# Low parts of the unsummed weight blocks: from a subtraction on VectorE to a negated copy on ScalarE and an accumulating DMA

## The chip, the cores and the metric

The kernel runs on one core of one Trainium2 chip. The metric is device time in microseconds (us) from the first to the last instruction of one execution, taken over several runs; lower is better. A change of about 0.2% is the least that a measurement of this kernel can tell from no change.

## The reference, cut to what matters

Two layers of a hybrid diffusion backbone over 512 latent and 256 context tokens, model width 1024. Each layer is a gated feed-forward network (FFN, inner width 2816), a mixing block (neighbourhood attention, windowed attention and a Fourier part between one input and one output projection), and a second FFN. Every dense product is in float32:

```python
def swiglu(h, w1, w2):
    gate, up = jnp.split(h @ w1, 2, axis=-1)
    return (jax.nn.silu(gate) * up) @ w2

def hybrid_layer(x, xc, mod, mod_c, ...):
    x = ffn_sublayer(x, mod, 0, ...)             # xc likewise
    ...                                          # mixing: h @ w_in, three mixers, o @ w_out
    x = ffn_sublayer(x, mod, 2, ...)
```

The weights are w1 (1024 x 5632) and w2 (2816 x 1024) of four FFNs, w_in (1024 x 2048) and w_out (1024 x 1024) of two layers, and w_mod, which gives the modulation rows.

## The kernel before, in words

TensorE multiplies in a reduced float32 format (fp32r). To keep float32 accuracy, each operand is split in two: the high part is the value rounded to fp32r, the low part is the value less its high part. A product is then three matmuls: high by high, high by low, low by high (`mm`, L693 is the line of the profile for all of them).

Weights stream through on-chip memory. `weights()` has two threads. `loads()` has the DMA queue of SP bring one weight tile of 128 x 1024 (512 KB) after another into one of 2 buffers `raw` (a third joins once the modulation rows are done). `split()` takes them in the same order and makes of each two blocks of 128 x 512. A block needs one of 8 slots (`W_BUFS`); a slot is two tiles, `wh` and `wl`. `block()` has ScalarE (ACT) copy the block into `wh`, rounded (L324), and `low()` has VectorE (DVE) subtract `wh` from the block into `wl` (L328); then `raw` may be loaded anew, and TensorE (PE) may use the block. The slot comes free when PE's last matmul with the block is done.

Most of the first projection of each FFN (77 of 88 column pairs, weights of the name "ws") uses a scheme with 7 products in place of 8 (`sums()`, `pair7()`). Its pair of tiles gives 7 blocks: three are parts of the weights themselves (a11, a12, a22), four are sums and differences (s1 to s4), which VectorE first writes into tiles `q` (L333). So VectorE and ScalarE convert 861 blocks in all: 308 from `q` and 553 straight from `raw` (3 of each of the 77 pairs, and all blocks of w2, w_in, w_out, the 11 other pairs of w1 and the Fourier tables). The blocks of the first modulation weights (32, L459 and L460) are converted elsewhere.

The order of all instructions on every engine is made by a planner (`Sched`) when the program is built: each step has an engine, an assumed duration and, for transfers, an assumed time until its result may be used (the last argument of `op`), and the step that could start first is put next. Engines then run their lists in order; an instruction that waits holds up all behind it on its engine. Slots and buffers are counted resources (`acq`, `rel`).

Other work that the change touches by sharing an engine: GpSimd (POOL) computes 1/sqrt of the norm (`rstd`, L547) at each start of a sublayer, and issues no DMA. ScalarE evacuates PSUM banks, computes silu (L935, L943) and makes the high parts of activations (L667). VectorE adds partial products (L1023), reduces the modulation rows from `wmodT` tiles (L433, which come by SP's queue, L427) and makes low parts of activations (L668). Ten small transfers (`gsd`, L533) turn a column of 1024 values into a row in DRAM.

Of the kernel before, what the change touches and what calls it, by code (L numbers as in the profile page):

```python
# [13 lines left out]
AF = mybir.ActivationFunctionType  # L14
ALU = mybir.AluOpType
# [143 lines left out]
def op(eng, dur, fn, extra=0.0):  # L159
    return ("op", eng, dur, fn, extra)  # L160


def wait(ev):
    return ("wait", ev)


def acq(name, n=1):
    return ("acq", name, n)


def t_dve(n, ap=False):
    return n / 960.0 + (0.13 if ap else 0.07)


def t_act(n, ap=False):
    return n / 1200.0 + (0.18 if ap else 0.09)
# [6 lines left out]
class Prog:  # L183
# [111 lines left out]
    def weights(self):  # L295


        nc, S = self.nc, self.S
        its = self.items()
        self.W = {}  # L300
        for k, _ in its:
            if k[0] == "ws":
                self.W.update({(*k, b): Event() for b in BLOCKS})
            else:
                self.W[k] = [Event() for _ in range(self.halves(k))]
        loaded = [[Event() for _ in aps] for _, aps in its]

        def loads():
            yield wait(self.start_w)
            for (key, aps), evs in zip(its, loaded):  # L310
                for ap, ev in zip(aps, evs):
                    yield acq("raw_w")
                    raw = self.rawp.tile([128, 1024], F32, name="raw")
                    n = 512 * self.halves(key)
                    yield op("sp", 1.45 * n / 1024, lambda: nc.sync.dma_start(out=raw[:, :n], in_=ap), 2.0)
                    S.set(ev, raw)

        def slot():
            wh = self.wp.tile([128, 512], F32R, name="wh")
            wl = self.wp.tile([128, 512], F32R, name="wl")  # L320
            return wh, wl

        def block(src, w, ev, after):
            yield op("act", t_act(512), lambda: nc.scalar.activation(w[0], src, AF.Copy))  # L324
            S.spawn(low(src, w, ev, after), 0)

        def low(src, w, ev, after):
            yield op("dve", t_dve(512), lambda: nc.vector.tensor_tensor(w[1], src, w[0].bitcast(F32), ALU.subtract))  # L328
            after()
            S.set(ev, w)  # L330

        def tt(o, a, b, f):
            return op("dve", t_dve(512), lambda: nc.vector.tensor_tensor(o, a, b, f))  # L333

        def sums(key, evs):
            rg = yield wait(evs[0])
            left = {0: 4, 1: 2}

            def done(*which):
                for r in which:  # L340
                    left[r] -= 1
                    if left[r] == 0:
                        S.rel("raw_w")

            a11, a12 = rg[:, :512], rg[:, 512:]
            W = lambda n: self.W[(*key, n)]
            yield acq("w")
            yield from block(a11, slot(), W("a11"), lambda: done(0))
            yield acq("w")
            yield from block(a12, slot(), W("a12"), lambda: done(0))  # L350
            ru = yield wait(evs[1])
            a21, a22 = ru[:, :512], ru[:, 512:]
            yield acq("q")
            s1 = self.qp.tile([128, 512], F32, name="q")
            yield tt(s1, a21, a22, ALU.add)
            yield acq("q")
            s2 = self.qp.tile([128, 512], F32, name="q")
            yield tt(s2, s1, a11, ALU.subtract)
            yield acq("w")
            yield from block(s1, slot(), W("s1"), lambda: S.rel("q"))  # L360
            yield acq("q")
            s4 = self.qp.tile([128, 512], F32, name="q")
            yield tt(s4, a12, s2, ALU.subtract)
            done(0)
            yield acq("w")
            yield from block(s2, slot(), W("s2"), lambda: S.rel("q"))
            yield acq("w")
            yield from block(s4, slot(), W("s4"), lambda: S.rel("q"))
            yield acq("q")
            s3 = self.qp.tile([128, 512], F32, name="q")  # L370
            yield tt(s3, a11, a21, ALU.subtract)
            done(0, 1)
            yield acq("w")
            yield from block(s3, slot(), W("s3"), lambda: S.rel("q"))
            yield acq("w")
            yield from block(a22, slot(), W("a22"), lambda: done(1))

        def split():
            for (key, _), evs in zip(its, loaded):
                if key[0] != "ws":  # L380
                    raw = yield wait(evs[0])
                    n = self.halves(key)
                    for i in range(n):
                        yield acq("w")
                        after = (lambda: S.rel("raw_w")) if i == n - 1 else (lambda: None)
                        yield from block(raw[:, i * 512 : i * 512 + 512], slot(), self.W[key][i], after)
                    continue
                yield from sums(key, evs)

        S.spawn(loads(), 0)  # L390
        S.spawn(split(), 0)

    @staticmethod
# [1458 lines left out]
```

## Time and profile before

| | us |
|---|---|
| median of 3 runs | 2574.09 |
| lowest and highest run | 2572.94, 2575.4 |
| the profiled execution | 2578.36 |
| its span, first to last instruction | 2576.6 |
| PE busy | 2518.8 (98%) |
| DVE busy | 1957.9 (76%) |
| ACT busy | 1266.8 (49%) |
| POOL busy | 68.1 (3%) |

The profile is of one execution. Busy time of an engine leaves out the time that it spends on waits and on issuing DMAs. PE is busy in every slice of the span but the first; that says that it always has a matmul under way, not that it could not be quicker. All later rows give times from the start of the span.

### The profile page before, as it was taken

How to read it: one execution, taken by the hardware profiler on the slowest of the kernel's cores; microseconds unless marked ns; L12 is line 12 of the kernel's file. 1: busy time of each engine (PE TensorE's matmuls, PEld its weight loads, DVE VectorE, ACT ScalarE, POOL GpSimd, SP SyncE). 2: the span in 40 equal slices, each digit the busy share in tenths (PEclk: the TensorE clock that was granted, in tenths of full speed). 3: DMA queues.
4: the chain of work that ended last, by engine and by line, in shares of the span. 5: the costliest groups of instructions: out<-in, count | busy, mean ns of one | idle time of the engine just before them, and what ended most of it. 6: DMA issues, size and time to landing. Idle time of an engine off the chain costs nothing.

```text
span 2576.6 us, 40296 instructions
## 1 busy us (share of the span) xinstructions
PE 2518.8 (98%) x15304; PEld 2291.8 (89%) x15304; DVE 1957.9 (76%) x3906; ACT 1266.8 (49%) x2529; POOL 68.1 (3%) x136
## 2 busy tenths in 40 slices
PE   7999999999999999999999999999999999999998
PEld 5989998998887899998999999899999877899998
DVE  7878888886888397887887968666667577768887
ACT  8433333356557474333334743333347566654544
POOL 0000000010000000000000100000001000000000
PEclk9999999999999999999999999999999999999999
DMA  6333434353321324344447344222243221333334
GB/s 255 95 119 123 127 121 103 117 196 102 123 62 34 123 86 129 121 131 107 123 123 201 118 156 155 75 74 69 71 154 112 69 68 67 114 115 91 99 107 131
DMA packets 100931, 294.17 MB, mean 114 GB/s; under 512 B 20608, under 2 KB 27136, under 8 KB 100608
## 3 DMA queue, kind: packets, MB, share of 16 engines
q1 hardware_dynamic: 100736, 291.59, 36.7%
q8 instruction: 120, 1.97, 0.3%
q14 instruction: 75, 0.61, 0.1%
HBM read 274.73 MB, written 16.82 MB: 113 GB/s over the span
## 4 chain that ended last, share of the span: by engine, by line
PE 90%; DVE 3%; DMA 3%; ACT 2%; issue 1%; SPq 0%; POOL 0%; DVEq 0%; POOLq 0%; ACTq 0%
PE b L693 82%; PE b L1345 3%; PE b L1388 2%; PE b L1324 2%; DMA raw<-wmodT 1%; PE b L675 1%; DMA raw<-w 1%; DVE wl L328 1%; ACT wh L324 1%; DMA raw<-win 1%; DMA g<-wmod 0%; DVE q L433 0%; ACT y L661 0%; DVE wl L460 0%; PE b L1134 0%
## 5 line engine op out<-in xcount | busy, mean ns | idle before, releaser
L693 PE MATMUL b<-hh,wh 128*128 128x256 f32 (+2 forms) x2184 | 703.4, 322 | 18.1 <-ACT q L935 13.2
L693 PE MATMUL b<-hl,wh 128*128 128x256 f32 (+2 forms) x2184 | 686.8, 318 | 1.7 <-DVE hl L668 1.4
L693 PE MATMUL b<-hh,wl 128*128 128x256 f32 (+2 forms) x2184 | 667.5, 318 | 0.0
L693 PE MATMUL b<-wh,g 128*128 128x512 f32 x1936 | 606.9, 390 | 0.0
L328 DVE TENSOR_TENSOR wl<-raw,wh 128x512 fp32r<-128x512 f32 x553 | 367.0, 689 | 132.1 <-ACT wh L324 129.7
L324 ACT ACTIVATE wh<-raw 128x512 fp32r<-128x512 f32 x553 | 336.4, 627 | 233.4 <-PE b L693 177.9
L693 PEld LDWEIGHTS b<-hh,wh 128*128 128x128 f32 x2184 | 414.4, 190 | 39.5 <-ACT q L935 14.2
L693 PEld LDWEIGHTS b<-wh,g 128*128 128x128 f32 x1936 | 363.6, 188 | 73.9
L693 PEld LDWEIGHTS b<-hl,wh 128*128 128x128 f32 x2184 | 414.4, 190 | 14.5 <-DVE hl L668 2.7
L693 PEld LDWEIGHTS b<-hh,wl 128*128 128x128 f32 x2184 | 402.4, 190 | 3.0
L324 ACT ACTIVATE wh<-q 128x512 fp32r<-128x512 f32 x308 | 190.5, 629 | 418.5 <-DVE y L1023 248.9
L693 PE MATMUL b<-wl,g 128*128 128x512 f32 x968 | 377.3, 390 | 0.0
L433 DVE CUSTOM_DVE_ANT_0 q<-raw,cb 128x1024 bf16<-128x1024 f32 x224 | 273.5, 1221 | 55.7 <-DMA raw<-wmodT 54.7
L693 PE MATMUL b<-x,wh 128*128 128x384 f32 (+1 forms) x1232 | 292.3, 323 | 0.0
L328 DVE TENSOR_TENSOR wl<-q,wh 128x512 fp32r<-128x512 f32 x308 | 206.3, 688 | 73.2 <-ACT wh L324 72.1
L1023 DVE TENSOR_TENSOR y<-y,b 128x512 f32<-128x512 f32 x264 | 179.6, 685 | 101.3 <-PE b L693 99.7
L693 PEld LDWEIGHTS b<-x,wh 128*128 128x128 f32 x1232 | 215.1, 189 | 0.0
L693 PEld LDWEIGHTS b<-wl,g 128*128 128x128 f32 x968 | 181.8, 188 | 35.8
L693 PE MATMUL b<-x,wl 128*128 128x384 f32 (+1 forms) x616 | 198.6, 322 | 0.0
L693 PE MATMUL b<-g,wh 128*128 128x384 f32 (+1 forms) x616 | 148.6, 327 | 4.3 <-ACT s L935 4.3
L961 ACT ACTIVATE g<-s 128x384 fp32r<-128x384 f32 (+1 forms) x154 | 75.5, 494 | 95.2 <-DVE s L948 94.1
L693 PEld LDWEIGHTS b<-x,wl 128*128 128x128 f32 x616 | 116.2, 189 | 0.0
(258 smaller groups left out, 3219.9 us busy)
## 6 DMA issues: line engine op xcount, KB each, us to landing
raw<-w SPq DMA_DIRECT2D x264, 512.0 KB, 3.6
raw<-wmodT SPq DMA_DIRECT2D x128, 512.0 KB, 3.6
raw<-win SPq DMA_DIRECT2D x32, 512.0 KB, 3.6
spill<-x SPq DMA_DIRECT2D x28, 512.0 KB, 2.9
x<-spill SPq DMA_DIRECT2D x26, 512.0 KB, 7.0
g<-wmod SPq DMA_DIRECT2D x32, 256.0 KB, 5.4
raw<-wout SPq DMA_DIRECT2D x16, 512.0 KB, 3.6
y<-bias SPq DMA_DIRECT2D x24, 256.0 KB, 3.1
```

What stands on the lines that cost most here:

```text
L324: yield op("act", t_act(512), lambda: nc.scalar.activation(w[0], src, AF.Copy))
L328: yield op("dve", t_dve(512), lambda: nc.vector.tensor_tensor(w[1], src, w[0].bitcast(F32), ALU.subtract))
L433: yield op("dve", t_dve(1024, True), lambda: nc.vector.tensor_tensor_reduce(junk, raw, self.cb[:, i, :], 1.0, 0.0, ALU.mult, ALU.add, self ...
L675: r = nc.tensor.transpose(bank[:, c : c + 128], yb[:, t, 2 * j + i, :], self.ident)
L693: mm = lambda *a, **k: self.nc.tensor.matmul(*a, skip_group_check=onto, **k)
L961: yield op("act", t_act(N), lambda: nc.scalar.activation(gh, ts[h], AF.Copy))
L1023: yield op("dve", t_dve(512), lambda: nc.vector.tensor_tensor(dst, dst, p, ALU.add))
L1324: r = nc.tensor.transpose(pb[:, j * 128 : j * 128 + 128], P[:, b * 128 : b * 128 + 128], self.ident)
L1345: r = nc.tensor.matmul(ps[b][:, c : c + w], lhsT=q[x], rhs=k[x], start=x == 0, stop=x == 1)
L1388: r = nc.tensor.matmul(po["t"][64 * h : 64 * h + 64, cols], lhsT=vs[h][j], rhs=Ps[h][:, j * 128 : j * 128 + 128], start=(j == 0), stop=(j ...
```

## The change

For the 553 blocks that come straight from `raw`, ScalarE makes a second copy, negated, into `wl`. The DMA queue of POOL then brings the same 128 x 512 values out of DRAM again and adds them onto `wl` (128 rows of 2 KB; an accumulating DMA). VectorE no longer takes part in these blocks. `raw` is released after the second copy. The 308 blocks from `q` stay as they are.

```diff
+        def added(src, ap, w, ev, after):
+            yield op("act", t_act(512), lambda: nc.scalar.activation(w[0], src, AF.Copy))
+            yield op("act", t_act(512), lambda: nc.scalar.activation(w[1], src, AF.Copy, scale=-1.0))
+            after()
+            S.spawn(add(ap, w, ev), 0)
+        def add(ap, w, ev):
+            yield op("pool", 1.0, lambda: nc.gpsimd.dma_start(out=w[1], in_=ap, accum_op=ALU.add), 2.5)
+            S.set(ev, w)
...
-        def sums(key, evs):
+        def sums(key, aps, evs):
...
-            yield from block(a11, slot(), W("a11"), lambda: done(0))
+            yield from added(a11, aps[0][:, :512], slot(), W("a11"), lambda: done(0))
...
-            yield from block(a12, slot(), W("a12"), lambda: done(0))
+            yield from added(a12, aps[0][:, 512:], slot(), W("a12"), lambda: done(0))
...
-            yield from block(a22, slot(), W("a22"), lambda: done(1))
+            yield from added(a22, aps[1][:, 512:], slot(), W("a22"), lambda: done(1))
...
-                        yield from block(raw[:, i * 512 : i * 512 + 512], slot(), self.W[key][i], after)
+                        cols = slice(i * 512, i * 512 + 512)
+                        yield from added(raw[:, cols], aps[0][:, cols], slot(), self.W[key][i], after)
```

## Rows read from the trace of the kernel before

**Rows 1.** The page's head and its first part: span, busy time by engine.

```profile
span 2576.6 us, 40296 instructions
PE 2518.8 (98%) x15304; PEld 2291.8 (89%) x15304; DVE 1957.9 (76%) x3906; ACT 1266.8 (49%) x2529; POOL 68.1 (3%) x136
```

**Rows 2.** Windows of 50 us: busy PE, PEld, DVE, ACT, POOL; clock, DMA share, GB/s.

```profile
250.00:300.00 50.00, 50.00 (x257) 45.74 (x256) 42.98 (x73) 16.27 (x30) 0.00 (x0) 1.00 0.38 115
1700.00:1750.00 50.00, 50.00 (x256) 45.75 (x256) 30.95 (x50) 16.80 (x31) 0.00 (x0) 1.00 0.22 64
```

**Rows 3.** The chain that ended last, shares by line (the answer cuts the line off).

```profile
by line: PE b L693 82.2%; PE b L1345 2.7%; PE b L1388 1.9%; PE b L1324 1.8%; DMA raw<-wmodT 1.2%; PE b L675 1.0%; DMA raw<-w 0.9%; issue 0.8%; DVE wl L328 0.6%; ACT wh L324 0.5%; DMA raw<-win 0.5%; DMA g<-wmod 0.4%; DVE q L433 0.4%; ACT y L
```

**Rows 4.** Costliest groups: the two conversions; busy us, mean ns, idle before.

```profile
L328 DVE TENSOR_TENSOR wl<-raw,wh 128x512 fp32r<-128x512 f32 x553 | 367.0, 689 | 132.1 <-ACT wh L324 129.7
L324 ACT ACTIVATE wh<-raw 128x512 fp32r<-128x512 f32 x553 | 336.4, 627 | 233.4 <-PE b L693 177.9
```

**Rows 5.** Waits: who waited for whom, us in total, times, longest.

```profile
SPq L315 <- DVE wl L328: 768.7, 198, 27.1
ACT wh L324 <- PE b L693: 243.9, 208, 9.5
```

**Rows 6.** Timeline: start, duration; ACT's conversions, then PE's matmuls with the low parts.

```profile
533.12 0.63 ACT L324 ACTIVATE wh<-raw 128x512 fp32r<-128x512 f32 x1 [1.18 <-DMA raw<-w]
563.56 1.99 ACT L324 ACTIVATE wh<-raw 128x512 fp32r<-128x512 f32 x3 [0.39 <-PE b L693]
570.33 1.14 ACT L324 ACTIVATE wh<-raw 128x512 fp32r<-128x512 f32 x2
873.64 0.63 ACT L324 ACTIVATE wh<-raw 128x512 fp32r<-128x512 f32 x1 [0.29 <-PE b L693]
1426.10 1.99 ACT L324 ACTIVATE wh<-raw 128x512 fp32r<-128x512 f32 x3 [0.48 <-PE b L693]
2548.39 0.63 ACT L324 ACTIVATE wh<-raw 128x512 fp32r<-128x512 f32 x1 [0.82 <-DMA raw<-w]
...
537.34 0.39 PE L693 MATMUL b<-wl,g 128*128 128x512 f32 x1
568.36 0.28 PE L693 MATMUL b<-hh,wl 128*128 128x256 f32 x1
574.01 0.28 PE L693 MATMUL b<-hh,wl 128*128 128x256 f32 x1
878.51 0.40 PE L693 MATMUL b<-wl,hh 128*128 128x512 f32 x1
1430.90 0.28 PE L693 MATMUL b<-hh,wl 128*128 128x256 f32 x1
2550.92 0.39 PE L693 MATMUL b<-wl,g 128*128 128x512 f32 x1
```

**Rows 7.** DMA: the queue's packets, MB, share; issues: count, KB each, us to landing.

```profile
q1 hardware_dynamic: 100736, 291.59, 36.7%
...
raw<-w SPq DMA_DIRECT2D x264, 512.0 KB, 3.6
...
y<-bias SPq DMA_DIRECT2D x24, 256.0 KB, 3.1
q<-gsd SPq DMA_DIRECT2D x20, 256.0 KB, 6.5
```

**Rows 8.** Timeline: one DMA issue of SP, two operations of POOL on one column.

```profile
562.37 0.32 SPq L640 DMA_DIRECT2D spill<-x  x1
...
570.59 0.86 POOL L547 TENSOR_TENSOR R<-r,nhalf 128x1 f32<-128x1 f32 x1 [9.82 <-DVE r L543]
573.14 2.74 POOL L547 TENSOR_TENSOR R<-r,nhalf 128x1 f32<-128x1 f32 x1 [1.69 <-DVE r L545]
```

**Rows 9.** Timeline of DVE: a late modulation row; a scaling of 1024 columns.

```profile
424.52 1.23 DVE L433 CUSTOM_DVE_ANT_0 q<-raw,cb 128x1024 bf16<-128x1024 f32 x1 [5.94 <-DMA raw<-wmodT]
...
572.19 0.75 DVE L635 TENSOR_SCALAR y<-x,R 128x1024 f32<-128x1024 f32 x1
```

More of the change, by code (lines that the diff above doesn't have):

```diff
@@ L375, in sums @@
             yield acq("w")
-            yield from block(a22, slot(), W("a22"), lambda: done(1))
+            yield from added(a22, aps[1][:, 512:], slot(), W("a22"), lambda: done(1))
         def split():
-            for (key, _), evs in zip(its, loaded):
+            for (key, aps), evs in zip(its, loaded):
                 if key[0] != "ws":
@@ L385, in split @@
                         after = (lambda: S.rel("raw_w")) if i == n - 1 else (lambda: None)
-                        yield from block(raw[:, i * 512 : i * 512 + 512], slot(), self.W[key][i], after)
+                        cols = slice(i * 512, i * 512 + 512)
+                        yield from added(raw[:, cols], aps[0][:, cols], slot(), self.W[key][i], after)
                     continue
-                yield from sums(key, evs)
+                yield from sums(key, aps, evs)
         S.spawn(loads(), 0)
```

## The prediction

> **What bounds the kernel now.** I read the busy times first, then the windows, the chain of waits, and last the timeline around the weight blocks. The busy times say that PE leaves only 2576.6 - 2518.8 = 57.8 us of the span idle [rows 1]. The windows say whether its busy time is work: in two windows of 50 us, 1450 us apart, it runs 257 and 256 matmuls, although DVE is busy for 42.98 us in the one and 30.95 in the other [rows 2]. The rate does not move with DVE's load, so inside the FFNs PE sets the pace and DVE's 76% bounds nothing. The chain agrees: matmuls are most of it, and the lines that the change touches, DVE's L328 and ACT's L324, hold 0.6% and 0.5% [rows 3]. So there is little to win, and the question is whether PE still finds its weights ready.
>
> What gives it time is the slots: ACT's conversion waited 208 times, 243.9 us in all, for PE to free one, and SP's loads waited 768.7 us for `raw` [rows 5]. A block is made as soon as a slot is free and used some blocks later. How much later is the number on which everything hangs. For each of the 547 of these 553 blocks that L693 uses I took, in the order of the timeline, the time from the end of ACT's write to the first matmul with its low part. The median is 13 us; but 23 blocks have under 6 us and 100 under 8. They sit where PE turns from one kind of work to the next and several slots come free at once. At the start of a mixing block ACT's write ends at 563.56 + 0.63 = 564.19 and PE wants the low part at 568.36: 4.2 us. The next pair is written at 570.33 + 0.63 = 570.96 and wanted at 574.01: 3.1 us. In the last chunk of an FFN it is 533.75 to 537.34, 3.6 us; at the output projection 874.27 to 878.51, 4.2 us; at the start of an FFN 1426.73 to 1430.90, 4.2 us; and just before the end 2549.02 to 2550.92, 1.9 us [rows 6].
>
> **The change part by part.**
>
> *Removed:* 553 subtractions of 689 ns, 367.0 us of DVE's busy time [rows 4]. PE's pace does not depend on them. On the chain L328 holds 0.6% of 2576.6 = 15.5 us [rows 3], of which 553/861 come from `raw`: -9.9 us.
>
> *Added on ACT:* 553 writes of 627 ns [rows 4], about 340 us; ACT goes from 49% to some 62%. It stays below PE, but its writes are on the chain too: L324 has 0.5% = 12.9 us, for 861 writes; the second write of 553 of them costs +8.3 us by the same share. Net of both -1.6 us, between -16 (all of L328's share goes and ACT's costs nothing) and +13 (the reverse).
>
> *Moved:* the low part is ready not one subtraction after ACT's write but after a longer path, L: the second write, POOL's issue, and the DMA. The second write comes 0.52 us after the first, as in the pair that takes 1.14 us in place of 0.63 [rows 6]. A hop between engines I estimate at 0.1, the subtraction's end being mostly under 1.3 us behind ACT's. POOL issues no DMA in this trace. SP's issue takes 0.32 us; POOL's cheapest work, an operation on one column, takes 0.86, and up to 2.74 [rows 8]. I take 0.9, since POOL spends that on next to nothing. The landing: plain 256 KB from SP takes 3.1 us, 512 KB 3.6, and 256 KB among other transfers 6.5 [rows 7]. An add must read 256 KB from DRAM and 256 KB from on-chip memory before it writes, and it runs beside the loads of `raw`; I take 4.7, between 3.1 and 6.5. So L = 0.52 + 0.1 + 0.9 + 4.7 = 6.2 us; at the low ends 0.52 + 0.1 + 0.32 + 3.1 = 4.0, at the high ends 9.9.
>
> What PE loses: each block whose time to use is under L makes PE late by the difference, unless an earlier delay has pushed the use (a block written after that delay is pushed as well and counts afresh). Carried through the 547 blocks in order with L = 6.2, 24 blocks count. The places: 2.6 us near 537; 2.0 + 3.1 + 0.4 at 568 to 580; 2.4 at 878; 3.6 at 911 to 921; 0.8 at 977; 3.0 at 1400; 2.0 + 1.7 at 1431 to 1438; 1.2 at 1916; 2.0 at 1947; 2.4 at 2196; 4.7 over the last blocks, 2547 to 2551; 0.3 at 38. Sum +32 us. The sum is steep in L: +5 us at 4.0, +17 at 5.2, +58 at 7.2, +122 at 8.8, +187 at 10, since the median block has only twice L.
>
> *The queues:* POOL's 553 issues of 0.9 us are 498 us of 2576; in pairs they come every 1.04 us (two ACT writes), so they don't pile up. The 1/sqrt of `rstd` waits behind them on POOL, at the starts of sublayers, where a few are on the path: +1 us, between 0 and 5. SP's queue loses nothing: `raw` is released after ACT's second write, 0.52 us behind the first, about when the subtraction ended. DMA engines: they are busy 36.7% of the span, 946 us [rows 7]. Between 1700 and 1750 they are busy 0.22 x 50 = 11 us for 64 GB/s x 50 us = 3.2 MB [rows 2], so 512 KB take 1.8 us of all 16. An add that reads 512 KB would take the same, 553 x 1.8 = 995 us: together 75%, hidden. At 250 to 300 there are 0.38 x 50 = 19 us, and 11 adds bring 20 more: that fits as well.
>
> *The late modulation rows:* DVE's L433 waits up to 5.94 us for a row at four or five places [rows 9], and PE's sums and additions wait behind it. Those stalls stay; blocks from `raw` no longer queue there, but PE needs the others too. No gain is counted.
>
> A rule of the Trainium skill speaks against the change beyond this. DVE's scaling of 1024 columns takes 0.75 us [rows 9] where a subtraction of 512 takes 0.69 [rows 4], so it runs in a faster mode. "SBUF — State Buffer", section "SBUF: two separate sides", says that such operations hold a port which POOL needs to write the descriptors of its own DMAs, so that these wait until it ends. By it an add at the start of a sublayer could be up to 0.75 us later, some +4 us over six starts. No row of this kernel shows it, and my sum leaves it out.
>
> *The sum* against the profiled execution: 2578.4 + 32 - 1.6 + 1 = 2609.8 us. The median of the runs shown is 2574.09, 4.3 us below that execution's 2578.36, so I forecast 2605 us, 1.2% slower. With L from 5.2 to 7.2 this case spans 2590 to 2631.
>
> **The rivals.**
>
> *The add lands like a plain transfer.* Then L is 4.0, PE loses 5 us, and if DVE's freed time is worth its whole share of the chain with ACT's writes hidden, the balance is 5 - 16 = -11: 2563 us. With the middle of the ACT and DVE terms it is +4: 2578. For it: 512 KB land only 0.5 us after 256 KB would, so bytes cost little. Against: an add has a read more, and POOL is slow at everything. It decides for faster from L below 4.5. The Trainium skill's "DMA: Bandwidth & Descriptors", section "Anatomy of one DMA — SWDGE (gpsimd) path", gives 2.0 us plus bytes over 436 GB/s for a DMA of POOL, 2.6 us here by my estimate, near the 3.1 us of rows 7; by it L would be 3.2 and the sum about 2574. It is stated for copies, not for adds.
>
> *The adds get in each other's way.* With L near 9 to 10, because POOL takes up to 2.7 us for an issue or an add lands in 6.5 us among three others, PE loses 120 to 187 us: 2695 to 2760. For it: transfers among others already take 6.5 us. Against: the mean distance of adds is 2576/553 = 4.7 us.
>
> *The DMA engines fill up.* If an add takes over 2.9 us of all 16 engines, (2576 - 946)/553, they bound the kernel; at 3.6, four times a plain 256 KB, the time is 946 + 553 x 3.6 = 2940 us. For it: nothing here shows how fast the engines add. Against: it takes more than 1.6 times my 1.8.
>
> *The planner makes another order of PE's list*, since durations change: the change then does not only do what it says. Some 10 us either way about 2578.
>
> **How the numbers follow.** Chances: forecast 0.50; plain landing 0.22 (0.14 faster, 0.08 within 0.2%); adds in each other's way 0.16; engines full 0.08; another order 0.04 (half of it faster). A change of 0.2%, 5 us, is the least that can be told from none. Faster: 0.14 + 0.02 = 0.16. Same: 0.08 + 0.02 from the forecast's low end = 0.10. Slower: 0.74. The range runs from 2566, in the plain-landing case, to 2720, in the middle of the third case; it leaves out about 0.19.
>
> **What would show it.** In the profile after: L328 from `raw` gone, DVE near 1590 us, ACT near 1610; the time from POOL's issue to landing near 4.7 us; PE idle or its first matmul with a low part late at the places listed, and PE's idle time near 90 us in place of 57.8. The forecast is wrong if the adds land within 3 us or need over 7, if the DMA share goes over 85%, or if PE waits at other places than these.

## The result and the profile after

| | before | after |
|---|---|---|
| median, us | 2574.74 (4 runs, 2572.94 to 2577.73) | 2815.55 (4 runs, 2804.38 to 2822.58) |
| span of the profiled execution | 2576.6 | 2820.5 |
| mean granted clock of TensorE | 0.990 | 0.966 |

The changed kernel takes 1.093 of the time before [1.0885, 1.0975], 241 us more. The forecast was 2605 us with a range to 2720; the direction was right, the size and the range were not. The nearest of the rivals is "the adds get in each other's way", and even its 2760 us is passed.

The page of the changed kernel: head, busy times (us, share of the span, instructions), queues (packets, MB, share of 16 engines' span), the two new groups (busy us, mean ns, idle time before), and DMA issues (count, KB each, median us from the start of the issue to the landing). Lines left out are marked by dots, here and below.

```profile
span 2820.5 us, 41695 instructions
...
PE 2604.3 (92%) x15304; PEld 2330.8 (83%) x15304; DVE 1632.3 (58%) x3350; ACT 1527.5 (54%) x3085; POOL 537.4 (19%) x689
...
q1 hardware_dynamic: 100736, 291.59, 33.0%
q0 software_dynamic: 79632, 145.00, 30.4%
...
L335 POOL DMA_DIRECT2D wl<-w x451 | 390.2, 871 | 1584.2 <-ACT wl L330 1455.1
...
L330 ACT ACTIVATE wl<-raw 128x512 fp32r<-128x512 f32 x553 | 341.0, 617 | 0.0
...
raw<-w SPq DMA_DIRECT2D x264, 512.0 KB, 5.8
wl<-w POOLq DMA_DIRECT2D x451, 256.0 KB, 7.0
raw<-wmodT SPq DMA_DIRECT2D x128, 512.0 KB, 4.7
```

Against [rows 1]: DVE lost 326 us of busy time and ACT gained 261, as intended (to 1632 and 1528; about 1590 and 1610 were forecast). But PE's idle time in the span, forecast near 90, went from 57.8 to 216.2 us (+158), and its busy time, with the same 15304 matmuls, from 2518.8 to 2604.3 (+85.5). The second number is for the most part the clock: a mean grant of 0.966 puts PE at the lower of its two levels, 1.2 in place of 2.4 GHz, for (1 - 0.966) / 0.5 x 2820 = 192 us, against 52 us before, and work at half pace for 140 us more costs up to some 70 us (up to, since part of those 140 us is idle). So about two thirds of the loss is PE waiting, and a third is PE working more slowly. Against [rows 7], a load of `raw` lands in 5.8 us in place of 3.6.

Who waited for whom, in the changed kernel (us in total, times, longest):

```profile
DVE q L445 <- DMA raw<-wmodT: 228.4, 93, 10.2
...
PEld b L705 <- DMA wl<-w: 89.7, 53, 5.3
...
PE b L705 <- DMA wl<-w: 69.9, 45, 4.9
...
PE b L705 <- ACT q L947: 42.6, 23, 7.5
...
PE b L705 <- DVE q L980: 21.2, 19, 3.6
```

The same view of the kernel before, for the two waits on loads that were not shown there:

```profile
DVE q L433 <- DMA raw<-wmodT: 54.7, 18, 9.3
...
ACT wh L324 <- DMA raw<-w: 39.9, 33, 9.1
```

PE now waits for the adds themselves (`DMA wl<-...`), DVE waits four times as long as before for the modulation rows, and PE then waits for what DVE and ACT make late (`q`). That leaves two theories. **The path**: a low part comes so much later than DVE's subtraction that PE gets there first. **The crowding**: 145 MB of adds slow the loads, the modulation rows come late, and PE waits for DVE. A third share may be neither: ACT's second write, and another order of the lists.

Windows of 50 us in the changed kernel (PE, PEld, DVE, ACT, POOL, clock, DMA share, GB/s):

```profile
400.00:450.00 50.00, 41.25 (x192) 37.33 (x191) 31.29 (x54) 19.77 (x38) 7.76 (x9) 0.90 0.70 172
1850.00:1900.00 50.00, 50.00 (x256) 45.75 (x256) 23.78 (x39) 22.51 (x42) 9.99 (x12) 1.00 0.54 123
2600.00:2650.00 50.00, 45.98 (x304) 42.19 (x303) 27.90 (x53) 27.88 (x60) 12.93 (x15) 0.97 0.72 165
```

In the middle window, in the first FFN of the second layer, twelve adds go by and PE runs its 256 matmuls as in [rows 2]: an add is not harmful as such. In the others the DMA engines are busy 70 to 72% and PE falls short.

### The profile page after: what moved, and what is told of

The parts are those of the page before. It is cut to its first block, busy times and chain, and to the rows that moved or that the text cites. A ratio compares the mean times of both kernels' runs of the same rounds, so it can differ in the third digit from the quotient of the medians.

```text
span 2820.5 us, 41695 instructions
## 1 busy us (share of the span) xinstructions
PE 2604.3 (92%) x15304; PEld 2330.8 (83%) x15304; DVE 1632.3 (58%) x3350; ACT 1527.5 (54%) x3085; POOL 537.4 (19%) x689
## 3 DMA queue, kind: packets, MB, share of 16 engines
q0 software_dynamic: 79632, 145.00, 30.4%
q8 instruction: 120, 1.97, 0.3%
## 4 chain that ended last, share of the span: by engine, by line
PE 58%; DMA 19%; issue 10%; DVE 7%; ACT 3%; POOL 2%; POOLq 0%; SPq 0%; DVEq 0%; ACTq 0%
PE b L705 50%; DMA wl<-w 6%; DMA raw<-wmodT 6%; DMA raw<-w 5%; POOL wl L335 2%; PE b L1357 2%; DVE q L445 2%; PE b L1336 2%; PE b L1400 2%; DVE q L344 1%; ACT wl L330 1%; DVE wl L339 1%; ACT wh L329 1%; PE b L687 1%; DMA wl<-win 1%
## 5 line engine op out<-in xcount | busy, mean ns | idle before, releaser
L705 PE MATMUL b<-hh,wh 128*128 128x256 f32 (+2 forms) x2184 | 715.7, 328 | 72.2 <-ACT q L947 42.6
L705 PE MATMUL b<-hh,wl 128*128 128x256 f32 (+2 forms) x2184 | 676.6, 322 | 31.9 <-DMA wl<-w 20.2
L705 PE MATMUL b<-hl,wh 128*128 128x256 f32 (+2 forms) x2184 | 693.9, 321 | 0.9 <-DVE hl L680 0.3
L335 POOL DMA_DIRECT2D wl<-w x451 | 390.2, 871 | 1584.2 <-ACT wl L330 1455.1
L705 PE MATMUL b<-wh,g 128*128 128x512 f32 x1936 | 617.9, 396 | 0.0
L329 ACT ACTIVATE wh<-raw 128x512 fp32r<-128x512 f32 x553 | 345.3, 624 | 234.1 <-DMA raw<-w 110.0
L324 ACT ACTIVATE wh<-q 128x512 fp32r<-128x512 f32 x308 | 192.5, 629 | 501.0 <-DVE y L1035 221.0
L705 PE MATMUL b<-wl,g 128*128 128x512 f32 x968 | 388.5, 401 | 50.1 <-DMA wl<-w 49.7
L705 PEld LDWEIGHTS b<-wh,g 128*128 128x128 f32 x1936 | 371.5, 192 | 74.8
L445 DVE CUSTOM_DVE_ANT_0 q<-raw,cb 128x1024 bf16<-128x1024 f32 x224 | 273.8, 1222 | 229.4 <-DMA raw<-wmodT 228.4
L330 ACT ACTIVATE wl<-raw 128x512 fp32r<-128x512 f32 x553 | 341.0, 617 | 0.0
L953 DVE TENSOR_TENSOR s<-s,b 128x384 f32<-128x384 f32 (+1 forms) x154 | 79.8, 518 | 102.8 <-PE b L705 82.9
```

The costliest lines, as they stand in the source:

```text
L330: yield op("act", t_act(512), lambda: nc.scalar.activation(w[1], src, AF.Copy, scale=-1.0))
L335: yield op("pool", 1.0, lambda: nc.gpsimd.dma_start(out=w[1], in_=ap, accum_op=ALU.add), 2.5)
L445: yield op("dve", t_dve(1024, True), lambda: nc.vector.tensor_tensor_reduce(junk, raw, self.cb[:, i, :], 1.0, 0.0, ALU.mult, ALU.add, self ...
L705: mm = lambda *a, **k: self.nc.tensor.matmul(*a, skip_group_check=onto, **k)
L953: yield op("dve", t_dve(N), lambda: nc.vector.tensor_tensor(ts[h], ts[h], src, ALU.add))
```

## The experiments

Each edit stands against the changed kernel unless it says otherwise. Each group of experiments below has runs of the kernel before on the same chip beside it; those had medians of 2578.4, 2573.72 and 2582.12 us in the three groups, and every difference is taken from the one of its own group.

### What a transfer adds

**No transfer.** All instructions and waits but the add:

```diff
-            yield op("act", t_act(512), lambda: nc.scalar.activation(w[1], src, AF.Copy, scale=-1.0))
+            yield op("act", t_act(512), lambda: nc.scalar.activation(w[1], src, AF.Copy, scale=0.0))
...
-            yield op("pool", 1.0, lambda: nc.gpsimd.dma_start(out=w[1], in_=ap, accum_op=ALU.add), 2.5)
+            yield op("pool", 1.0, lambda: None, 2.5)
```

> The changed kernel without its 553 adds: ACT writes both parts (the second scaled by 0, so the low parts are left at zero), POOL issues nothing, all orders as the planner made them. Theory A (PE waits for adds that land late, 7.0 us in the median) and theory B (the adds crowd the 16 DMA engines and slow the other loads) both expect the whole loss of 241 us gone: 2560 to 2600 us, DVE's wait for wmodT rows back near 55 us. Theory C (ACT's second write and the planner's new order are what costs) expects 2700 us or more.

Measured: 2633.6 us, 1.0205 [1.0183, 1.0228], so +55 us with no transfer at all. That is more than the path or the crowding expected (2560 to 2600 us) and far less than the third theory did (2700 or more). What remains is ACT's second write and the planner's new order.

**A narrow add.** The same, and the add moves 16 of the 512 columns:

```diff
+            yield op("pool", 1.0, lambda: nc.gpsimd.dma_start(out=w[1][:, :16], in_=ap[:, :16], accum_op=ALU.add), 2.5)
```

> The changed kernel with the add cut to the first 16 of 512 columns (64 bytes a row; ACT's second write scaled by 0, so the other low parts are zero): the same path of second write, POOL's issue and landing, a thirty-second of the bytes. Theory A in its plain form (the path's length is what costs, whatever the bytes) expects a landing over 5 us and 2640 us or more. Theory B expects landing near 3.5 to 4.5 us and 2580 to 2600 us, as my list of places gives +9 to +15 us for a path of 4.5 to 5 us. Theory C expects over 2700 us.

Measured: 2665.8 us, 1.033 [1.0307, 1.0352]: +87, that is +32 over no transfer. The same number of issues and of packets (79632), almost no bytes. The landing takes 3.6 us, as the crowding expected, but the time is one that the path expected: neither had both right. Carrying these blocks' measured paths through the timeline of the kernel without a transfer, as the prediction did, gives +32 us as well.

**A plain copy.** Full width, without the addition:

```diff
-            yield op("pool", 1.0, lambda: nc.gpsimd.dma_start(out=w[1], in_=ap, accum_op=ALU.add), 2.5)
+            yield op("pool", 1.0, lambda: nc.gpsimd.dma_start(out=w[1], in_=ap.bitcast(F32R)), 2.5)
```

> The changed kernel with a plain DMA in place of the add: POOL copies the weights over the negated copy (the low parts are wrong), same rows of 2 KB, same waits, but one read less. If the adding is what makes it slow, landing falls from 7.0 to about 4.5 us and the time to 2600 to 2650 us (theory A by a faster landing, theory B by a third less load). If POOL's way of issuing and the shared engines matter and not the adding, landing stays over 6 us and the time over 2750 us.

Measured: 2724.81 us, 1.0559 [1.0531, 1.0587]: +146. Its page:

```profile
q0 software_dynamic: 79632, 145.00, 18.9%
...
L335 POOL DMA_DIRECT2D wl<-w x451 | 240.0, 532 | 1654.4 <-ACT wl L330 1548.8
...
wl<-w POOLq DMA_DIRECT2D x451, 256.0 KB, 4.9
```

The bytes of the queue are those of the changed kernel, but they take 18.9% of the engines' time in place of 30.4%, land in 4.9 us in place of 7.0, and POOL's issue takes 0.53 us in place of 0.87. So the addition costs 241 - 146 = 95 us of the loss, by POOL's issue, by its landing and by its time of the engines. Landing and time came out between the two cases that were expected (4.5 us and at most 2650; over 6 us and 2750): the addition is a part of the loss, and a copy would be slow too. The edit also reads the source as fp32r, the type of the tile; a conversion is not what makes the difference, as the adds of the next experiment, float32 onto float32, take the same 178 ns for a packet of 2 KB as those of the changed kernel (medians; 99 ns in the plain copy).

**Traffic alone.** The kernel before, with DVE's subtractions and as many adds of the same size beside them, onto scratch tiles in DRAM that nobody waits for:

```diff
         def block(src, w, ev, after, traffic=False):
             yield op("act", t_act(512), lambda: nc.scalar.activation(w[0], src, AF.Copy))
             S.spawn(low(src, w, ev, after), 0)
+            if traffic:
+                S.spawn(extra(w), 0)
+        def extra(w):
+            ...
+            yield op("pool", 1.0, lambda: nc.gpsimd.dma_start(out=scratch[i % 8], in_=w[0].bitcast(F32), **kw), 2.5)
```

> The kernel before, with 553 accumulating DMAs of 256 KB from POOL that nobody waits for: each adds the high part just written onto one of 8 scratch tiles in DRAM (the first 8 copy). The matmuls get their low parts from DVE as before. Theory B expects most of the loss without any wait for an add: 2650 to 2750 us, raw loads landing in 5 to 6 us, DVE waiting over 150 us for wmodT rows. Theory A expects under 2600 us, since no matmul waits for an add. Theory C expects the time of before plus at most 15 us.

Measured: 2669.22 us, 1.0352 [1.0329, 1.0375]: +91 us. Here nobody waits for an add, so this is crowding without the path (with the direction turned: on-chip to DRAM, and in an order that the planner changed a little: 416 of PE's 15304 matmuls stand elsewhere). `raw` lands in 6.0 us, and DVE waits 126.6 us for modulation rows, where over 150 were expected. Matmul by matmul against the kernel before, 77 of the 97 us that the profiled execution loses lie before 1640 us, while modulation rows are loaded: in the midst of FFNs 10.3 us at 180 to 405, 13.0 at 930 to 1190, 12.0 at 1230 to 1395. The loss is 0 at 1640 to 1910 and 0.3 at 2260 to 2540, where none are loaded. Crowding falls short of the whole.

The last of these stretches tells the two theories apart. It is shown for the kernel before, for the traffic alone and for the full add in the order of before (below), each time for the same matmuls, some 1960:

```profile
2260.00:2540.00 280.00, 280.00 (x1963) 262.84 (x1962) 221.74 (x404) 144.38 (x303) 0.00 (x0) 1.00 0.33 101
2350.00:2630.00 280.00, 280.00 (x1961) 262.23 (x1960) 221.56 (x403) 143.69 (x303) 77.36 (x90) 1.00 0.83 186
2426.00:2757.00 331.00, 302.21 (x1967) 273.87 (x1966) 169.50 (x314) 186.67 (x394) 78.40 (x90) 0.94 0.71 158
```

With the DMA engines busy 83% and nobody waiting for an add, PE does not lose a microsecond; with PE waiting for the adds, at 71%, the same work takes 51 us longer. Here the crowding of the loads is worth nothing, and the path (with ACT's second write, worth 5 us in this stretch, and a granted clock of 0.94 in place of 1.00) is worth all.

### The same with the order of before

The planner orders anew whenever a duration changes, which blurs the parts. So ACT's second write, and POOL's issue behind it, were put where DVE's subtraction stood in the plan: PE's, SP's and DVE's other instructions keep the order of the kernel before.

**No transfer, order of before.**

```diff
+            S.spawn(add(src, ap, w, ev, after), 0)
+        def add(src, ap, w, ev, after):
+            def second():
+                nc.scalar.activation(w[1], src, AF.Copy, scale=0.0)
+            yield op("dve", t_dve(512), second)
+            after()
```

> As e1_no_transfer (two writes on ACT, the second scaled by 0, no adds), but ACT's second write stands where the planner had put DVE's subtraction: the lists of PE, SP and POOL are those of the kernel before, word for word. If the new order cost e1 its 55 us, this comes back to 2570 to 2590 us, a little faster than before if DVE's 380 us were worth anything. If ACT's second write holds up ACT's other work, it stays at 2620 us or more.

Measured: 2611.03 us, 1.0146 [1.0127, 1.0165]: +37. That is the move of the write from DVE to ACT, alone; it lies between the two cases expected (2570 to 2590, and 2620 or more), so the write and the new order both had a part in the 55 us. PE's waits (us in total, times, longest):

```profile
PE b L707 <- ACT q L949: 17.9, 10, 6.0
PE b L513 <- ACT wh L473: 10.0, 1, 10.0
PE b L707 <- ACT hh L681: 9.9, 3, 6.8
```

and of the kernel before, for the same three:

```profile
PE b L693 <- ACT q L935: 13.2, 3, 6.3
PE b L499 <- ACT wh L459: 10.1, 1, 10.1
...
PE b L693 <- ACT hh L667: 4.2, 2, 3.1
```

PE waits longer for ACT's evacuations (`q`) and for the high parts of activations (`hh`), which stand behind the second writes in ACT's list. PE's idle time is 80.0 us in place of 57.8, and its busy time 18.2 us longer at a granted clock of 0.985. By place, 12.4 of the 40.4 us that the profiled execution loses lie at 2100 to 2260 and 5.5 at 880 to 930, and 0 to 0.4 in the midst of the FFNs at 180 to 405 and 1640 to 1910.

**Narrow add, order of before** (`nc.gpsimd.dma_start(out=w[1][:, :16], in_=ap[:, :16], accum_op=ALU.add)` behind the write in `second`).

> As f1_order_no_transfer, with the add of the first 16 of 512 columns issued right behind ACT's second write (the other low parts are zero). The list of PE is that of before, so the list of places of the prediction applies: with a landing of 3.6 us, as in e8_narrow_add, the path L is 4.4 us and PE loses 8 us: f1 plus 5 to 15 us. If a path of this length costs more than my list says, f1 plus 30 us or more.

Measured: 2653.07 us, 1.0304 [1.0289, 1.032]: +42 over the one without a transfer. From the end of ACT's first write to the landing is 5.4 us by the median; the list of blocks gives +58 for the measured paths. The 4.4 us and the +5 to +15 that were expected had left out that ACT's second write stands later in this order: it ends 1.05 us behind the first by the median, in place of 0.52.

**Full add, order of before** (the same with all 512 columns and the scale -1.0).

> The changed kernel with full adds in the order of the kernel before. If the loss is the late adds and the crowded engines, whatever the order, it stays within 30 us of the changed kernel: 2785 us or more. If the new order's 55 us simply come off, 2750 to 2770 us. By my list of places alone, with L = 7.8 us (0.5 + 0.3 + 7.0), f1 plus 78 us, some 2655 us; what is above that is the slowed loads and the clock.

Measured: 2812.77 us, 1.0926 [1.0902, 1.0949], the same as the changed kernel within the intervals: beside the adds, the changed kernel's new order is worth nothing that can be seen. It is +160 over the narrow add and +202 over no transfer, and PE waits more for the adds than for anything else (PE and its weight loads):

```profile
PEld b L707 <- DMA wl<-w: 126.5, 75, 5.3
...
DVE q L447 <- DMA raw<-wmodT: 114.6, 55, 8.8
PE b L707 <- DMA wl<-w: 94.4, 63, 5.1
```

DVE's wait for modulation rows is half that of the changed kernel (228.4) and `raw` lands in 4.4 us in place of 5.8, at the same time in all: how much the loads are crowded hangs on the order, and the loss does not follow it. The list of blocks gives +178 over no transfer for the measured paths (5% of them under 5.8 us, median 8.65, 5% over 12.9), of which 178 - 58 = 120 come from the bytes.

The output projection of the second layer, one of the kinds of place that the prediction named, shows how. First POOL's adds, then PE's matmuls that had to wait (start, duration, operation, idle time before and who ended it):

```profile
2334.91 0.86 POOL L335 DMA_DIRECT2D wl<-wout  x1 [7.84 <-PE b L707]
2335.93 0.86 POOL L335 DMA_DIRECT2D wl<-wout  x1 [0.16 <-issue]
2336.98 1.75 POOL L335 DMA_DIRECT2D wl<-wout  x2 [0.18 <-ACT y L1676]
2346.11 0.86 POOL L335 DMA_DIRECT2D wl<-wout  x1 [7.38 <-PE b L707]
2347.67 0.86 POOL L335 DMA_DIRECT2D wl<-wout  x1 [0.70 <-ACT wl L334]
2348.71 1.75 POOL L335 DMA_DIRECT2D wl<-wout  x2 [0.18 <-ACT y L1676]
```

```profile
2347.36 0.40 PE L707 MATMUL b<-wh,hh 128*128 128x512 f32 x1
2347.60 0.39 PE L707 MATMUL b<-wl,hh 128*128 128x512 f32 x1
...
2350.42 0.52 PE L707 MATMUL b<-wl,hh 128*128 128x512 f32 x1 [1.97 <-DMA wl<-wout]
...
2352.65 0.80 PE L707 MATMUL b<-wl,hh 128*128 128x512 f32 x1 [0.86 <-DMA wl<-wout]
2353.24 0.63 PE L707 MATMUL b<-wh,hl 128*128 128x512 f32 x1
2353.67 0.63 PE L707 MATMUL b<-wh,hh 128*128 128x512 f32 x1
...
2355.51 0.80 PE L707 MATMUL b<-wl,hh 128*128 128x512 f32 x1 [1.22 <-DMA wl<-wout]
...
2357.85 0.80 PE L707 MATMUL b<-wl,hh 128*128 128x512 f32 x1 [0.69 <-DMA wl<-wout]
```

POOL issues four adds within 3.8 us. By the trace's landing times they land 5.2, 8.3, 9.8 and 12.6 us after their issue; the last releases PE at 2350.42. The next four land 6.5, 7.8, 9.1 and 10.4 us after theirs, one every 2.1 to 2.9 us, and each releases PE once (three are shown). A second thing is seen in the durations: ahead of the waits a matmul takes 0.39 us and the next starts 0.24 us after it; behind them it takes 0.63 and the next starts 0.43 after it (the first after an idle stretch takes 0.80). That is PE's clock: from 2330 to 2347.6 us, with PE busy throughout, the granted clock is 1.00; from 2350.4 to 2360, behind the first wait of 1.97 us, it is 0.52, near the lower level of 1.2 GHz.

**The planner is told the truth.** The changed kernel with POOL's step at 0.9 us and 6.1 us until the result may be used:

```diff
-            yield op("pool", 1.0, lambda: nc.gpsimd.dma_start(out=w[1], in_=ap, accum_op=ALU.add), 2.5)
+            yield op("pool", 0.9, lambda: nc.gpsimd.dma_start(out=w[1], in_=ap, accum_op=ALU.add), 6.1)
```

> The changed kernel, the planner told that POOL's issue takes 0.9 us and the result comes 6.1 us later (it assumed 1.0 and 2.5): the same instructions in another order. If an order made for adds that land too early is part of the loss, 2750 to 2790 us. If orders don't matter beside the adds, 2800 to 2830 us.

Measured: 2787.2 us, 1.083 [1.0813, 1.0847]: 28 us better than the changed kernel, as expected if an order made for adds that land early is part of the loss. The rest stays: this plan wins back a tenth of it.

### The modulation rows, and what could be won at most

**Few modulation bytes, before and with the add.** In both, a modulation row is loaded for 16 of its 1024 columns and DVE reads one column 1024 times, so that DVE's work stays and 66 MB of loads go. The first is the kernel before, the second the full add in the order of before:

```diff
-            yield op("sp", 1.45, lambda: nc.sync.dma_start(out=raw, in_=d["wmodT"][l, j]), 2.0)
+            yield op("sp", 1.45, lambda: nc.sync.dma_start(out=raw[:, :16], in_=d["wmodT"][l, j, :, :16]), 2.0)
...
-                    junk, raw, self.cb[:, i, :], 1.0, 0.0, ALU.mult, ALU.add, self.mod[l, s][:, j : j + 1]))
+                    junk, raw[:, :1].to_broadcast([128, 1024]), self.cb[:, i, :], 1.0, 0.0, ALU.mult, ALU.add, self.mod[l, s][:, j : j + 1]))
```

> The kernel before, with each modulation tile cut to 16 of its 1024 columns on the way in (64 bytes a row; VectorE reads the first column 1024 times, so the modulation rows are wrong): 128 loads of 512 KB less on the DMA engines, all lists as before. All theories: 2555 to 2580 us, as PE sets the pace; some of the four or five stalls behind a late modulation row may go. It is the base for h2_add_few_mods.

> f2_order_add (full adds, the order of before) with the modulation tiles cut in the same way. Theory B (inside the FFNs adds, weight loads and modulation loads together crowd the DMA engines; f2_order_add lost 63 us there between 180 and 1610 us of the kernel before, and nothing between 1640 and 1910, where no modulation rows are loaded) expects that part gone: h0 plus 150 to 185 us. If the path of the adds costs this whatever else is loaded, h0 plus 220 us or more.

Measured: 2565.57 us, 0.9941 [0.9924, 0.9959], and 2779.63 us, 1.077 [1.0749, 1.0792]. With the loads that crowding was to make late almost gone, the add still costs 2779.63 - 2565.57 = 214 us; with them it cost 2812.77 - 2573.72 = 239. The crowding of the modulation rows is worth some 25 us. What the crowding theory expected here (150 to 185) is missed by 29 us, the path's 220 or more by 6: it is mostly the path, with some crowding in it. The second kernel's waits and landing:

```profile
PEld b L707 <- DMA wl<-w: 114.1, 64, 4.9
PE b L707 <- DMA wl<-w: 86.7, 58, 4.5
```

```profile
raw<-w SPq DMA_DIRECT2D x264, 512.0 KB, 4.4
wl<-w POOLq DMA_DIRECT2D x451, 256.0 KB, 6.4
```

PE waits for adds as before, and these still take 6.4 us. When the modulation rows no longer hold PE up, it runs into the late low parts instead.

**No low parts.** The order of before, the write and the add left out, and PE reads the high part twice:

```diff
+            def second():
+                return None
+            yield op("dve", t_dve(512), second)
+            after()
+            S.set(ev, (w[0], w[0]))
```

> f1_order_no_transfer without ACT's second write: the 553 blocks have no low part, PE reads the high part in its place, DVE has no subtraction for them; order of before. If f1's 37 us come from ACT's second write at the starts of sublayers, 2560 to 2575 us, and what it is below 2574 is all that DVE's freed 380 us can bring. If they come from elsewhere, 2600 us or more.

Measured: 2577.13 us, 0.9981 [0.9972, 0.9991]. Freeing DVE of 367 us, at no cost anywhere, is worth 5 us. With the lists in this order, no way of making the low parts elsewhere can win more; another order, made for a free DVE, was not tried.

**POOL subtracts.** The subtraction itself goes to POOL, no DMA:

```diff
+        def plow(src, w, ev, after):
+            yield op("pool", 1.3, lambda: nc.gpsimd.tensor_tensor(w[1], src, w[0].bitcast(F32), ALU.subtract))
+            after()
```

> The kernel before with the 553 subtractions on POOL in place of DVE: no second write on ACT, no transfer, DVE freed, the planner told 1.3 us each. If POOL takes about 1.3 to 1.6 us and nobody else is held up, the path is 1 us longer than before: 2565 to 2590 us. If POOL and DVE get in each other's way or POOL needs over 2.5 us, POOL's list becomes late: over 2620 us. It would be the better version if DVE's freed time is worth more than the longer path.

Measured: 2650.58 us, 1.0267 [1.0249, 1.0286]. A subtraction takes POOL 1.49 us where DVE took 0.69 [rows 4]:

```profile
L333 POOL TENSOR_TENSOR wl<-raw,wh 128x512 fp32r<-128x512 f32 x553 | 813.4, 1489 | 1585.3 <-ACT wh L329 1500.7 <-PE b L1334 30.5 <-PE b L703 16.9
```

Better than the adds, still slower than the kernel before, and slower than the 2565 to 2590 us expected for a subtraction of 1.3 to 1.6 us. The other condition that was named for a loss did come true: POOL and DVE get in each other's way. DVE is busy for 1900.7 us, against 1629.6 without low parts and with nearly the same other work. These are two of its groups without low parts, and then the same two while POOL subtracts:

```profile
L1037 DVE TENSOR_TENSOR y<-y,b 128x512 f32<-128x512 f32 x264 | 180.0, 686 | 128.6 <-PE b L707 128.0
...
L976 DVE TENSOR_TENSOR g<-s,g 128x384 fp32r<-128x384 f32 (+1 forms) x154 | 80.0, 523 | 54.0 <-ACT g L975 53.7
```

```profile
L1033 DVE TENSOR_TENSOR y<-y,b 128x512 f32<-128x512 f32 x264 | 178.6, 685 | 92.1 <-PE b L703 91.8
...
L972 DVE TENSOR_TENSOR g<-s,g 128x384 fp32r<-128x384 f32 (+1 forms) x154 | 132.4, 859 | 67.5 <-ACT g L971 66.5
```

The operation that has neither operand in a PSUM bank takes 859 ns in place of 523; the one that reads a bank (`b`) takes what it took. Not every operation of the first kind suffers as much: DVE's subtractions from `q` take 711 ns in place of 689. How the loss divides into this and the planner's new order, no run separates. No kernel of this series that does the whole work beat the kernel before.

## Why the prediction was right in kind and wrong in size

The ladder in the order of before gives the parts of the loss (239 us there, 241 in the changed kernel):

| step | us |
|---|---|
| ACT writes the second part, in DVE's place | +37 |
| issue and landing of an add of few bytes | +42 |
| the bytes and the addition | +160 |
| the planner's new order, in their presence | about 0 |

**What bounds the kernel** held. PE's pace does not hang on DVE's load: without the low parts the kernel gains only 5 us. The -9.9 us for the removed subtractions was twice too much.

**The second write was mis-sized**: +8.3 us forecast, +13 at most, +37 measured (with DVE's relief in it). What failed here is the price by a share of the chain, L324's 12.9 us scaled by the count. Such a share tells what the writes cost now; it does not tell what stands behind them in ACT's list. At the starts of sublayers these are the evacuations and the high parts of activations for which PE waits.

**The path L was mis-sized, and this is the step that failed most.** The second write and the hop were near: 0.52 us; ACT's end to POOL's start 0.29 us where I took 0.1. From there to the landing I took 0.9 + 4.7 = 5.6 us. The measured landing counts from the start of POOL's issue, whose 0.86 us it holds, and has a median of 7.0; in the changed kernel 5% land under 4.7 us, 17% under 5.6 and 5% over 11.2. So the landing itself, after the issue, is 6.1 where I took 4.7. (The rows that I took 4.7 from count SP's issue of 0.32 us too, so L held an issue more than once; by luck that brought it nearer.) The median L is 7.8 us where I had 6.2, and a fifth of the paths are over the 9.9 of my high ends. One value for all blocks was wrong besides: the delays follow the late ones, and blocks near each other in time are late together. On my own list a path of 7.8 us gives +76; on the list of the kernel without a transfer, the median of the full add, 8.65 us, given to every block makes +141 us, each block's own L +178, and measured are +202.

**The list** held in part. In the order of before it gives 58 and 178 us against 42 and 202 measured. In the planner's new order, over the kernel without a transfer, it gives 32 us for the narrow add (32 measured), but 57 for the plain copy against 91, and 121 for the changed kernel against 186. The nearness of 178 to 202 is in part luck: the list counts waiting alone, and PE's idle time grew by 121.5 us there, the rest being slower work. One count of the prediction was wrong: 39 blocks, not 23, have under 6 us (23 have under 5); the sums of the list don't rest on it.

**Why the landing is long**: an add that finds no other in flight lands in 5.9 us by the median, with one in flight 6.6, two 7.2, three 8.0, four 10.2. I had counted the adds as 4.7 us apart on the average and so as rarely meeting; they come in groups, as slots come free in groups, and most find another one in flight. So even alone an add is 0.3 us over my 5.6, and most of the rest comes where others are in flight. My rival had the mechanism, but set its price from the landing of a single load among three; its path of 9 to 10 us is over the median, so that its time was passed too shows that other terms were missing from it as from the forecast. From issue to the first packet of data 4.0 us pass by the median (the queue's packets taken in order, 128 to an add), and the transfer itself starts its packets within 2.1 us. In the narrow add, with as many packets and next to no bytes, the same stretch is 2.2 us, in the plain copy 2.4: so some 1.6 to 1.8 of the 4.0 us come with the bytes and the addition, most likely those of adds ahead.

**Time of the engines** held: an add takes 0.304 x 2820.5 / 553 = 1.55 us of all 16, I had 1.8. But "together 75%, hidden" was wrong in the conclusion: at 64% in all, loads of `raw` already take 5.8 us in place of 3.6, and DVE's stalls at modulation rows, which I let stay as they were, grew from 54.7 to 228.4 us (95.2 without any transfer, by the new order alone). In effect this is the smaller part, since removing those loads gave back 25 us.

**Another order of PE's list** was a rival at some 10 us either way. Without transfers it costs 55 - 37 = 18 us; beside the adds it is not seen.

**The queue of POOL** did not pile up, as forecast: issues stand 1.04 us apart at the closest 5%, 1.94 by the median, and POOL starts 0.29 us after ACT in all but a few.

**The clock** is missing from my sum. A wait of PE for a low part costs more than its length when the matmuls behind it follow each other every 0.43 us in place of 0.24. Of the full add's 190.6 us of span over the kernel without a transfer (both in the order of before), 121.5 are idle time of PE and 69.1 are longer busy time, at a granted clock of 0.964 in place of 0.985.

The time that the Trainium skill's "DMA: Bandwidth & Descriptors", section "Anatomy of one DMA — SWDGE (gpsimd) path", gives for a DMA of POOL, 2.6 us by my estimate for 256 KB, is not reached in this setting: POOL's plain copies landed in 4.9 us, and only the quickest 5% in under 2.9. For collective operations, "Collectives: The Full Stack" of the Trainium skill, section "The bandwidth ceiling: the fold count and why AG ≠ RS ≠ AR", says that a reducing transfer is slow not for its arithmetic but because it reads two sources where a copy reads one, and gives a measured ratio of 1.93. The ratio here is near it: a packet of 2 KB takes 178 ns in an add and 99 ns in the plain copy (medians), 1.8 times; that the second read is the reason, no run here shows.

What stays open: what makes up the 24 us (order of before) and 65 us (changed kernel) by which the measured loss passes the list, since slower loads and the lost clock bring each other; whether DVE's faster operations hold up POOL's issues, which no run here isolates; and whether more slots would hide the adds, which was not tried.

## What to carry to other kernels

Before work is moved off an engine, price its removal alone: here a kernel without these operations gained 5 us, so a longer path had next to nothing to win. For a step that moves from an engine to a DMA, make the list of slacks (ready to wanted) and run it with a spread of landing times taken from transfers that meet each other, not with one value; the places where several buffers come free at once are where the transfers meet. Add to each wait of PE the slower clock behind it.

## What the runs showed of the hardware that was not expected

- An accumulating DMA from POOL costs more than a copy of the same bytes everywhere: POOL's issue 0.87 us against 0.53, landing 7.0 us against 4.9 from the start of the issue, 1.55 us of all 16 engines for 256 KB against 0.189 x 2724.1 / 553 = 0.93.
- An add of 8 KB still lands only after 3.6 us, though it moves a 32nd of the bytes (in as many packets).
- Adds issued about 1 us apart landed one every 2.1 to 4.1 us.
- With the DMA engines busy 83% of a stretch of 280 us, PE lost nothing, as long as it waited for no add.
- While POOL subtracts, DVE's operations with neither operand in PSUM take longer, to a different degree (859 ns for 523, 711 for 689); the one shown that reads PSUM does not (685 for 686). Beside the adds the first keeps its time (522 ns).
